# Reordering casts, gate products and exponentials in a fused hybrid decoder layer, and a seven-product form for its first pooling pair

## The chip, the cores and the metric

The kernel runs on one core of one Trainium2 chip. The metric is device time in microseconds (us), from launch to end; lower is better. A core has five engines that work side by side, each in the order of its own instruction queue: TensorE (PE in the profile, its weight loads PEld) multiplies matrices into PSUM, VectorE (DVE) and ScalarE (ACT) do elementwise work, GpSimd (POOL) does little but issue DMAs here, and SyncE (SP) issues DMAs. An instruction waits at the head of its queue until what it needs is there, and all behind it wait too.

## The reference

One decoder layer on 512 tokens and 16 leading meta tokens, width 1024, in float32:

```python
u = rmsnorm(h, mix_norm_w)
proj = u @ w_in                       # pool 1024, z 2048, x/B/C 4096, dt 32, gates 2048
y_pool = pool_mixer(u_pool, ...) @ w_pool_up
y_ssd = mamba2_branch(z, xbc, dt_raw, ...) @ w_ssd_out
h = h + (gate_pool * y_pool + gate_ssd * y_ssd) @ w_o
v = rmsnorm(h, mlp_norm_w)
h = h + relu(v @ w_ff1) ** 2 @ w_ff2
out = rmsnorm(h, final_norm_w)[:, 16:]
```

The Mamba branch has 8 groups of 256 channels. Each group goes through a causal convolution with silu (x, B, C), a chunked scan (four chunks of 128 tokens, with decays that are exponentials of running sums), a product with silu(z), and a norm over the group's 256 channels. The pooling branch has four groups with windows 2, 4, 8 and 16: the mean over the window minus the input, then a 256x256 product.

## The kernel before

Every float32 operand of TensorE is split into a high and a low part of a faster type. For weights, a block of 128x1024 is loaded by SP into a `raw` buffer, ACT casts it to the high half (`whi`, line 103), and DVE subtracts to get the low half (`wlo`, line 105). A product is then three matmuls: high times high, high times low input, low times high. There are four buffers for `whi`, four for `wlo` and three for `raw` (a fourth during the scan). A load waits until the low half of an older block has been taken, and a cast waits until TensorE has used up the high half of an older block.

The program is written with Python generators and a planner at compile time puts each engine's instructions into a fixed order, by the order of the text and by its own estimates of when operands are ready. `tc.issue_after(ins)` is a hint to that planner: the instructions in its block are placed behind `ins` in the queue of `ins`'s engine. It makes no wait of its own.

The scan part runs over the groups `g = 0..7`. `weave` (line 712) lets `ssd(g)`, the scan of one group, take turns with `group_proj(g + 1)`, the projections of the next group: first B and C (`plain`, lines 521 to 527), then x, then for three groups a pooling gate (`gate_pool`), then the two halves of z (`z_half`, line 529, into the PSUM tile `pz`). For groups 4 to 7 the x projection is a `pair` (line 480): two tiles of 256 channels are computed at once with seven half-size products instead of eight, in the order `b11 b21 t2 t1 s3 b22 t4`, on sums of the input that were prepared earlier (tiles `t0h`, `t1h` and their low parts) and on sums of the weights that GpSimd's DMAs accumulate in DRAM. The results of `pair` are combined by ACT and DVE from the PSUM tile `pqx` into `rax` and `rbx`.

`ssd(g)` is a generator of several steps: transposes of B and x (`ptb`, `ptm`, `ptx`), exponentials `eb` of the running sums and relus that prepare the decay mask (lines 612 to 626), the mask's exponentials (`decay`, line 627), the product of C and B (`pcb`, line 640), the chunk states (`st`, lines 656 and 657), the outputs (`po`, `py`, `yt`), the squares of the output (`sqg`) with their high and low half (`qhg`, line 319, and `qlg`, line 320), their sum over channels by TensorE (`png`, lines 693 and 694), and the normalized output's halves (`yh`, `yl`). Groups 0 to 3 also prepare the input's sums, in `sums_of_u` (line 876). With group 7 there is no next projection; `out_part` (line 822) takes its place and begins the branch's output projection (`psp`).

After the scan comes the pooling branch: `pool_tile` (line 931) for the two tiles of the first pool (window 16), products of the last two output blocks (`psl`), a gate, and `pool_pair` (line 963), the seven-product form, for the other three pools, where the weights' sums are made by DVE.

Of the kernel before, what the change touches and what calls it, by code (L numbers as in the profile page):

```python
# [64 lines left out]
def kernel(ctx: ExitStack, tc, xT, x, w, fx, f1, f2, vec, fnw, out):  # L65
# [32 lines left out]
        block_load(t, c)  # L98
        block_split(t, c)

    def block_split(t, c, behind=None):
        b, raw, hi, lo = t
        act.copy(hi[:, c], raw[:, c])  # L103
        with tc.issue_after(behind.ins) if behind is not None else nullcontext():
            dve.tensor_tensor(lo[:, c], raw[:, c], hi[:, c].bitcast(F32), op=ALU.subtract)  # L105

    def block(behind=None):
        t = block_tiles()
        block_load(t, slice(0, 1024))
        block_split(t, slice(0, 1024), behind)  # L110
        return t[2:]

    def raw_block():
# [82 lines left out]
        for o, c in outs:  # L196
            pe.matmul(o, wl, rhs[0][k][:, c], start=False, stop=k == NK - 1)

    def proj(outs, wblk, rhs):

        for part in range(2):
            for k in range(NK):
                wt = wblk[part][:, k * P : (k + 1) * P]
                for o, c in outs:
                    pe.matmul(o, wt, rhs[0][k][:, c], start=part == 0 and k == 0, stop=part == 1 and k == NK - 1)  # L205
                    if part == 0:
                        mm[0] = pe.matmul(o, wt, rhs[1][k][:, c], start=False, stop=False)  # L207

# [9 lines left out]
    def narrow(ps):  # L218
        return [(ps, slice(NM, L))]
# [95 lines left out]
    def col_sums(name, qt, n2, tags, bufs=1):  # L315

        qh = n2.tile(list(qt.shape), F32R, tag=tags[0], name=f"qh{name}", bufs=bufs)
        ql = n2.tile(list(qt.shape), F32R, tag=tags[1], name=f"ql{name}", bufs=bufs)
        act.copy(qh, qt)
        dve.tensor_tensor(ql, qt, qh.bitcast(F32), op=ALU.subtract)  # L320
        return qh, ql

# [138 lines left out]
    def pair_operands(i):  # L461
# [3 lines left out]
        for a in range(0, 7, 2):  # L465
# [11 lines left out]
            for j in range(len(ms)):  # L477
                yield hi[:, 512 * j : 512 * (j + 1)], lo[:, 512 * j : 512 * (j + 1)]

    def pair(kind, g, r):  # L480

        ps = psum2(f"pq{kind}{g}")
        banks = (ps[:, :HALF], ps[:, 512 : 512 + HALF])
        operands = pair_operands(PAIRS.index((kind, g)))
        one, two = HF
        for m, f, n, start, stop in MULTIPLY:
            o = banks[n]
            wt = next(operands)
            f = factor_u(f)
            for low in range(2):  # L490
                for k in range(4):
                    wk = wt[low][:, k * P : (k + 1) * P]
                    pe.matmul(o, wk, f[k][0], start=start and not low and k == 0,  # L493
                              stop=stop and low == 1 and k == 3, skip_group_check=True)
                    if not low:
                        pe.matmul(o, wk, f[k][1], start=False, stop=False, skip_group_check=True)
            if m == "b11":
                act.copy(r[0][:, one], o)
            elif m == "b21":
                dve.tensor_tensor(r[0][:, one], r[0][:, one], o, op=ALU.add)  # L500
            elif m == "t2":
                act.activation(r[1][:, one], o, AF.Copy, scale=-1.0)
            elif m == "t1":
                act.copy(r[1][:, two], o)
                yield
            elif m == "s3":
                dve.tensor_tensor(r[1][:, two], r[1][:, two], o, op=ALU.subtract)
            elif m == "b22":
                dve.tensor_tensor(r[1][:, one], r[1][:, one], o, op=ALU.add)
            else:  # L510
                act.copy(r[0][:, two], o)
# [4 lines left out]
    def group_proj(g, cur, gate=None):  # L516

        first = g == 0
        xc, bt, ct, zt = cur

        def plain(dst, t, skip):
            if first and (dst is bt or dst is ct):
                view = viewB if dst is bt else viewC
            else:
                runs, view = wide(psum2(f"px{g}_{t}"), skip)
                proj(runs, block(), X if first else U)
            conv(dst, first_raw(t, view, skip) if first else view, t)

        def z_half(ps, i):

            with tc.issue_after(done[0].ins) if g == 1 else nullcontext():
                wt = block()
            proj(narrow(ps), wt, X if first else U)

        bcs = ((bt, 16 + g, 0), (ct, 24 + g, NM - 4))
        xs = ((xc[:, 0, :], 2 * g, 0), (xc[:, 1, :], 2 * g + 1, 0))
        both = g in BC_PAIRS
        for kind, ts, paired in (("b", bcs, both), ("x", xs, g in X_PAIRS)):
            if paired:
# [37 lines left out]
    def ssd(g, cur):  # L577
# [31 lines left out]
        xdd = gs.tile([P, 3, R, 64], F32, tag="xdd", name=f"xdd{g}")  # L609
        x_decayed[g] = dve.tensor_tensor(xdd, xdt[:, :3, :, :], bc(dec[:, :3, hs], 64), op=ALU.mult)  # L610

        eb = gs.tile([P, 2, SEQ], F32, tag="eb", name=f"eb{g}")
        ap = abc.rearrange("p (i j) l -> p i j l", j=2)
        for j in range(2):
            js = slice(64 * j, 64 * j + 64)
            with tc.issue_after((z_ready if g in X_PAIRS else x_ready)[g].ins):
                act.activation(eb[js, :, :], ap[js, :, j, :], AF.Exp)
        dm = abc.rearrange("p r (c l) -> p r c l", c=4)
        for r in range(R):
# [15 lines left out]
        yield  # L635

        pc = psum1(f"pcb{g}")
        with tc.issue_after(filled[g].ins) if g in X_PAIRS and g in filled else nullcontext():
            for c in range(4):
                pe.matmul(pc[:, c * P : (c + 1) * P], bt[:, tok(c)], ct[:, ctok(c)], start=True, stop=True)  # L640
        cbm = gs.tile([P, 4, P], F32, tag="cbm", name=f"cbm{g}")
# [12 lines left out]
                decay()  # L654
        for c in range(3):
            dve.tensor_tensor(st[c + 1], st[c], bc(cdec[:, c, hs], 64), op=ALU.mult)
            dve.tensor_tensor(flat(st[c + 1]), flat(st[c + 1]), pv[c + 1], op=ALU.add)
        for rs_ in ((slice(0, 2), slice(2, R)) if g == G - 1 else (slice(0, R),)):
            n = rs_.stop - rs_.start
            masked[g] = dve.tensor_tensor(dm[:, rs_], dm[:, rs_], cbm.unsqueeze(1).to_broadcast([P, n, 4, P]),  # L660
# [25 lines left out]
        sq = gs.tile([P, 2, SEQ], F32, tag="eb", name=f"sqg{g}")  # L686
        squared[g] = act.activation(sq, yt, AF.Square)
        dve.tensor_tensor(sq[:, 0, :], sq[:, 0, :], sq[:, 1, :], op=ALU.add)
        qh, ql = col_sums(f"g{g}", sq[:, 0, :], gs, ("btok", "cbm"))
        mark[0] = qh.bitcast(F32)[:, :1]  # L690
        yield
        pn = psum1(f"png{g}")
# [14 lines left out]
            ys.append((yh, yl))  # L707
        yield

    done, abc_load, masked, y_first, squared, b_meta, x_decayed = {}, {}, {}, {}, {}, {}, {}  # L710

    def weave(a, b, n, sums, side):
# [109 lines left out]
    def out_part():  # L822

        def get(n):
            t = block_tiles()
            block_load(t, slice(0, 1024))

            with tc.issue_after(b_meta[G - 1].ins) if n == 1 else nullcontext():
                act.copy(t[2], t[1])
            with tc.issue_after(x_decayed[G - 1].ins) if n == 1 else nullcontext():  # L830
                dve.tensor_tensor(t[3], t[1], t[2].bitcast(F32), op=ALU.subtract)
            return t
# [43 lines left out]
    def sums_of_u(g):  # L876
# [11 lines left out]
            load(0)  # L888
        yield
        a, b = u_raw[g]  # L890
        with tc.issue_after(masked[g].ins):
            dve.tensor_tensor(b[:, two], a[:, two], b[:, two], op=ALU.subtract)
            dve.tensor_tensor(a[:, two], a[:, one], a[:, two], op=ALU.subtract)
            dve.tensor_tensor(a[:, one], b[:, two], a[:, one], op=ALU.subtract)
# [32 lines left out]
    pool_stack = ExitStack()  # L927
    gp = pool_stack.enter_context(tc.tile_pool(name="gp", bufs=2, side="right", reuse_waits="tile"))
    yps, last, copied, mixed = {}, {}, {}, []

    def pool_tile(t):
        win = WIN[t // 2]
        ps = psum2(f"pp{t}")

        skip = min(NM - win, NM - 4)
        runs, view = wide(ps, skip)
        proj(runs, block(), U)
        u = gp.tile([P, L + 8], F32, tag="pu", name=f"pu{t}", bufs=4)[:, :L]
        act.copy(u[:, skip:], view)
        return averaged(t, u)  # L940

    def averaged(t, u):
        win = WIN[t // 2]
# [92 lines left out]
    for _ in range(SETS_POOL):  # L1036
        with tc.issue_after(t_load.ins):
            t_load = weight_sums()
    pend = [pooled_halves(*pool_tile(2 * POOL_ORDER[0] + i)) for i in range(2)]

    un = units()
    psl_add = []
# [781 lines left out]
```

## Time and profile before

| what | value |
|---|---|
| time, median of 3 runs (lowest to highest) | 1010.49 us (1010.44 to 1011.99) |
| time of the profiled execution | 1010.66 us |
| span of its instructions | 1009.0 us |
| busy: PE, DVE, ACT, POOL | 993.8, 798.2, 604.8, 129.4 us |
| granted TensorE clock, mean of the span | 0.997 |

A line of the timeline gives the start in us from the span's start, the duration, the engine with the program line, the operation, output and inputs, and in brackets how long the engine had been idle before and what ended that. A line of the windows gives a stretch, its length, and for each engine asked for the busy time with the number of instructions, then the granted clock of TensorE (1.00 is full speed), the share of the DMA engines in use, and GB/s. Matmuls of one kind overlap in their pipeline, so that their distance and not their duration is what one costs.

### The profile page before, as it was taken

The page shows a single profiled execution, that of the slowest core. Times are in us where ns is not written, and L with a number is a line of the kernel's source. Part 1 is how long each engine was busy: PE and PEld are TensorE (multiplying, and loading weights), DVE is VectorE, ACT ScalarE, POOL GpSimd, SP SyncE. Part 2 cuts the span into 40 slices and gives each one's busy share as a digit, 9 for nine tenths or more (in the row PEclk, how much of TensorE's full clock was granted, in tenths as well). Part 3 has the DMA queues.
Part 4 walks back from the last instruction along what each step waited for, and adds up shares of the span by engine and source line. Part 5 has one row for each costly group of instructions (what it writes and reads, how often), then busy time and mean ns, then how long its engine had stood idle before and what let it go on. Part 6 is the DMA issues. An engine that isn't in the chain of part 4 may idle for free.

```text
span 1009.0 us, 15702 instructions
## 1 busy us (share of the span) xinstructions
PE 993.8 (98%) x6047; PEld 875.5 (87%) x6047; DVE 798.2 (79%) x1153; ACT 604.8 (60%) x853; POOL 129.4 (13%) x215
## 2 busy tenths in 40 slices
PE   9999999999999999999999999999999999999997
PEld 7889998998888898978999888888889999999986
DVE  7978897968754788988689657876988878888885
ACT  8657759494834566675345434368656656665654
POOL 0001331212122212213300000221000000000000
PEclk9999999999999999999999999999999999999999
DMA  7273958576889749478823631979355464554432
GB/s 250 90 262 100 314 175 218 170 207 201 225 226 271 211 129 276 138 210 203 258 94 122 225 124 64 290 197 345 86 190 154 137 200 135 167 173 153 135 106 83
DMA packets 61803, 184.52 MB, mean 183 GB/s; under 512 B 7072, under 2 KB 8416, under 8 KB 60704
## 3 DMA queue, kind: packets, MB, share of 16 engines
q1 hardware_dynamic: 39456, 109.00, 32.3%
q0 software_dynamic: 18240, 67.51, 26.0%
q10 hardware_dynamic: 4032, 7.00, 1.9%
q8 instruction: 47, 0.77, 0.3%
q14 instruction: 28, 0.23, 0.1%
HBM read 173.13 MB, written 58.59 MB: 230 GB/s over the span
## 4 chain that ended last, share of the span: by engine, by line
PE 90%; DVE 3%; ACT 3%; DMA 2%; issue 1%; SPq 0%; ACTq 0%; DVEq 0%
PE px L1443 8%; PE px L205 7%; PE alpha L1511 6%; PE pz L205 6%; PE px L1446 4%; PE px L207 3%; PE alpha L1514 3%; PE pz L207 3%; PE pgs L205 3%; PE pgp L205 2%; DMA raw<-in_w 2%; PE pqx L493 2%; PE pso L137 1%; PE wo_alpha L1205 1%; PE pf L138 1%; PE pf L137 1%
## 5 line engine op out<-in xcount | busy, mean ns | idle before, releaser
L103 ACT CAST whi<-raw 128x1024 fp32r<-128x1024 f32 (+2 forms) x90 | 90.0, 1011 | 87.5 <-DMA raw<-in_w 15.8
L105 DVE TENSOR_TENSOR wlo<-raw,whi 128x1024 fp32r<-128x1024 f32 (+2 forms) x90 | 104.7, 1172 | 37.6 <-ACT whi L103 21.1
L205 PE MATMUL px<-uh,whi 128*128 128x264 f32 (+1 forms) x320 | 80.9, 291 | 0.0
L207 PE MATMUL px<-ul,whi 128*128 128x264 f32 (+1 forms) x320 | 78.8, 285 | 0.0
L1218 DVE TENSOR_TENSOR ht<-ht,alpha 128x1024 f32<-128x1024 f32 x35 | 42.7, 1220 | 29.1 <-PE alpha L1511 29.1
L1141 ACT CAST shi<-rawf 128x1024 fp32r<-128x1024 f32 x42 | 44.2, 1053 | 28.7 <-PE alpha L1514 18.2
L205 PEld LDWEIGHTS px<-uh,whi 128*128 128x128 f32 x320 | 60.4, 189 | 1.1 <-issue 0.7
L207 PEld LDWEIGHTS px<-ul,whi 128*128 128x128 f32 x320 | 60.2, 188 | 0.2
L1511 PE MATMUL alpha<-shi,hh 128*128 128x512 f32 x140 | 55.2, 394 | 0.0
L1514 PE MATMUL alpha<-shi,hl 128*128 128x512 f32 x140 | 54.7, 391 | 0.0
L1142 DVE TENSOR_TENSOR slo<-rawf,shi 128x1024 fp32r<-128x1024 f32 x42 | 51.2, 1219 | 0.6 <-ACT shi L1141 0.6
L1446 PE MATMUL px<-vsl,shi 128*128 128x256 f32 x192 | 47.4, 280 | 0.0
L1443 PE MATMUL px<-vsh,shi 128*128 128x256 f32 x192 | 47.4, 281 | 0.0
L205 PE MATMUL pz<-uh,whi 128*128 128x512 f32 x112 | 44.2, 394 | 1.9 <-ACT yh L705 1.3
L207 PE MATMUL pz<-ul,whi 128*128 128x512 f32 x112 | 43.7, 390 | 0.0
L205 PE MATMUL px<-uh,wlo 128*128 128x264 f32 (+1 forms) x320 | 41.8, 283 | 0.0
L205 PEld LDWEIGHTS px<-uh,wlo 128*128 128x128 f32 x320 | 40.0, 188 | 0.2
L1511 PE MATMUL alpha<-slo,hh 128*128 128x512 f32 x140 | 37.4, 389 | 0.0
L698 DVE RECIPROCAL rs<-rs 128x128 f32<-128x128 f32 x32 | 27.2, 911 | 12.5 <-ACT rs L696 12.4
L1443 PEld LDWEIGHTS px<-vsh,shi 128*128 128x128 f32 x192 | 36.2, 188 | 0.9
L1446 PEld LDWEIGHTS px<-vsl,shi 128*128 128x128 f32 x192 | 36.1, 188 | 0.9
L1446 PE MATMUL px<-vl,shi 128*128 128x256 f32 x144 | 36.1, 283 | 0.0
(599 smaller groups left out, 3089.6 us busy)
## 6 DMA issues: line engine op xcount, KB each, us to landing
raw<-in_w SPq DMA_DIRECT2D x96, 512.0 KB, 4.6
f_t<-in_f POOLq DMA_DIRECT2D x38, 512.0 KB, 6.8
f_s<-in_f POOLq DMA_DIRECT2D x26, 512.0 KB, 7.0
b<-in_f SPq DMA_DIRECT2D x21, 512.0 KB, 4.6
rawf<-in_f SPq DMA_DIRECT2D x36, 256.0 KB, 3.0
rawf<-f_t SPq DMA_DIRECT2D x36, 256.0 KB, 2.9
abc<-acs_d POOLq DMA_DIRECT2D x8, 1024.0 KB, 7.6
f_t<-f_t POOLq DMA_DIRECT2D x12, 512.0 KB, 7.0
```

The costliest lines, as they stand in the source:

```text
L103: act.copy(hi[:, c], raw[:, c])
L105: dve.tensor_tensor(lo[:, c], raw[:, c], hi[:, c].bitcast(F32), op=ALU.subtract)
L205: pe.matmul(o, wt, rhs[0][k][:, c], start=part == 0 and k == 0, stop=part == 1 and k == NK - 1)
L207: mm[0] = pe.matmul(o, wt, rhs[1][k][:, c], start=False, stop=False)
L698: dve.reciprocal(rs[:, ctok(c)], rs[:, ctok(c)])
L1141: splits.append((act.copy(hi, src), dve.tensor_tensor(lo, src, hi.bitcast(F32), op=ALU.subtract)))
L1142: dve.tensor_tensor(lo, src, hi.bitcast(F32), op=ALU.subtract)))
L1218: added[0] = dve.tensor_tensor(o, o, src, op=op)
L1443: pe.matmul(ps, m, f[k][0], start=start and not low and k == 0, stop=stop and low == 1 and k == 3, skip_group_check=True)
L1446: pe.matmul(ps, m, f[k][1], start=False, stop=False, skip_group_check=True)
L1511: pe.matmul(ps[t], hh[:, p, seg, st], m, start=bool(first and not low and p == 0), stop=bool(last and low and p == 1), skip_group_check=True)
L1514: pe.matmul(ps[t], hl[:, p, seg, st], m, start=False, stop=False, skip_group_check=True)
```

## The change

Six edits, most of them hints to the planner; a small helper `after` takes several such hints at once:

- **z's casts**: for the three groups with a pooling gate among the projections (groups 2, 3 and 4), both casts of z's weights are placed behind `qhg` of the scan that runs beside them.
- **z's products**: for groups 4 to 7, the first matmul of z is placed behind the last matmul of the pair's third product (`t2`).
- **the last group's exponentials**: `ssd(7)` gets one more step, and its `eb` exponentials are placed behind the cast of `out_part`'s second weight block.
- **C times B**: `pcb` is placed behind the first projection of the next group for all groups that have one, and not only for groups 4 to 6.
- **sums of the input**: they are placed behind the last chunk state of the group, besides behind its mask.
- **the first pool** uses `pool_pair`; `pool_tile` goes away.

```diff
-    def block_split(t, c, behind=None):
+    def block_split(t, c, behind=None, cast_behind=None):
         b, raw, hi, lo = t
-        act.copy(hi[:, c], raw[:, c])
+        with after(cast_behind):
+            act.copy(hi[:, c], raw[:, c])
...
+    def proj(outs, wblk, rhs, behind=None):
...
-                    pe.matmul(o, wt, rhs[0][k][:, c], start=part == 0 and k == 0, stop=part == 1 and k == NK - 1)
+                    with after(behind if part == 0 and k == 0 else None):
+                        pe.matmul(o, wt, rhs[0][k][:, c], start=part == 0 and k == 0,
+                                  stop=part == 1 and k == NK - 1)
...
             elif m == "t2":
+                second_product[g] = at
...
             with tc.issue_after(done[0].ins) if g == 1 else nullcontext():
-                wt = block()
-            proj(narrow(ps), wt, X if first else U)
+                wt = block(None, halved.get(g - 1) if gate is not None else None)
+            proj(narrow(ps), wt, X if first else U, None if i else second_product.get(g))
...
+        if g == G - 1:
+            yield
         eb = gs.tile([P, 2, SEQ], F32, tag="eb", name=f"eb{g}")
...
-            with tc.issue_after((z_ready if g in X_PAIRS else x_ready)[g].ins):
+            with after((z_ready if g in X_PAIRS else x_ready)[g], late_cast[0] if g == G - 1 else None):
                 act.activation(eb[js, :, :], ap[js, :, j, :], AF.Exp)
...
-        with tc.issue_after(filled[g].ins) if g in X_PAIRS and g in filled else nullcontext():
+        with tc.issue_after(filled[g].ins) if g in filled else nullcontext():
...
-            dve.tensor_tensor(flat(st[c + 1]), flat(st[c + 1]), pv[c + 1], op=ALU.add)
+            last_state[g] = dve.tensor_tensor(flat(st[c + 1]), flat(st[c + 1]), pv[c + 1], op=ALU.add)
...
-        qh, ql = col_sums(f"g{g}", sq[:, 0, :], gs, ("btok", "cbm"))
+        qh, ql, halved[g] = col_sums(f"g{g}", sq[:, 0, :], gs, ("btok", "cbm"))
...
-            with tc.issue_after(b_meta[G - 1].ins) if n == 1 else nullcontext():
-                act.copy(t[2], t[1])
+            with after(b_meta[G - 1] if n == 1 else None):
+                cast = act.copy(t[2], t[1])
+            if n == 1:
+                late_cast[0] = cast
...
-        with tc.issue_after(masked[g].ins):
+        with after(masked[g], last_state[g]):
             dve.tensor_tensor(b[:, two], a[:, two], b[:, two], op=ALU.subtract)
...
-    pend = [pooled_halves(*pool_tile(2 * POOL_ORDER[0] + i)) for i in range(2)]
+    pend = [pooled_halves(*a) for a in pool_pair(POOL_ORDER[0])]
```

The pool pair, which the first pool now goes through, in its core:

```python
        a1, a2 = raw_block(), raw_block()
        fa = split_form(a1, both, f"A{p}")
...
            dve.tensor_tensor(sm[:, h1], a1[:, h1], a2[:, h1], op=ALU.add)
...
            dve.tensor_tensor(sm[:, h2], sm[:, h1], a2[:, h2], op=ALU.add)
        fs = split_form(sm, both, f"S{p}")
        dve.tensor_tensor(a1[:, h1], a2[:, h1], a2[:, h2], op=ALU.add)
        dve.tensor_tensor(a1[:, h2], a1[:, h2], sm[:, h2], op=ALU.add)
        fd = split_form(a1, both, f"D{p}")
        fb = split_form(a2, h2, f"B{p}")
...
        product(c, fa, 0, "A11", True, False)
        act.copy(r1[:, one], c)
        product(y, fa, 1, "A12", True, True)
        dve.tensor_tensor(r1[:, one], r1[:, one], y, op=ALU.add)
        product(c, fs, 1, "S2", False, False)
        act.activation(r2[:, one], c, AF.Copy, scale=-1.0)
        product(z, fs, 0, "S1", True, False)
        copied[p] = act.copy(r2[:, two], z)
        product(c, fd, 0, "S3", False, False)
        dve.tensor_tensor(r2[:, two], r2[:, two], c, op=ALU.subtract)
        product(z, fb, 1, "S4", False, True)
        dve.tensor_tensor(r2[:, one], r2[:, one], z, op=ALU.add)
        second = averaged(2 * p + 1, r2)
        product(c, fd, 1, "A22", False, True)
        act.copy(r1[:, two], c)
        return [averaged(2 * p, r1), second]
```

Each `product` is 4 input blocks times 3 matmuls of 264 columns; `pool_tile` had 8 input blocks times 3 matmuls times 2 runs of 264 columns for each of two tiles.

More of the change, by code (lines that the diff above doesn't have):

```diff
@@ L99, in block_part, with after, block @@
         block_split(t, c)
-    def block_split(t, c, behind=None):
+    def after(*ins):
+        st = ExitStack()
+        for i in ins:
+            if i is not None:
+                st.enter_context(tc.issue_after(i.ins))
+        return st
+    def block_split(t, c, behind=None, cast_behind=None):
         b, raw, hi, lo = t
-        act.copy(hi[:, c], raw[:, c])
+        with after(cast_behind):
+            act.copy(hi[:, c], raw[:, c])
         with tc.issue_after(behind.ins) if behind is not None else nullcontext():
             dve.tensor_tensor(lo[:, c], raw[:, c], hi[:, c].bitcast(F32), op=ALU.subtract)
-    def block(behind=None):
+    def block(behind=None, cast_behind=None):
         t = block_tiles()
         block_load(t, slice(0, 1024))
-        block_split(t, slice(0, 1024), behind)
+        block_split(t, slice(0, 1024), behind, cast_behind)
         return t[2:]
@@ L197, in proj_step @@
             pe.matmul(o, wl, rhs[0][k][:, c], start=False, stop=k == NK - 1)
-    def proj(outs, wblk, rhs):
+    def proj(outs, wblk, rhs, behind=None):
         for part in range(2):
@@ L318, in col_sums @@
         ql = n2.tile(list(qt.shape), F32R, tag=tags[1], name=f"ql{name}", bufs=bufs)
-        act.copy(qh, qt)
+        at = act.copy(qh, qt)
         dve.tensor_tensor(ql, qt, qh.bitcast(F32), op=ALU.subtract)
-        return qh, ql
+        return qh, ql, at
     NT = L // 6
@@ L478, in pair_operands @@
                 yield hi[:, 512 * j : 512 * (j + 1)], lo[:, 512 * j : 512 * (j + 1)]
+    second_product, halved = {}, {}
     def pair(kind, g, r):
@@ L492, in pair @@
                     wk = wt[low][:, k * P : (k + 1) * P]
-                    pe.matmul(o, wk, f[k][0], start=start and not low and k == 0,
-                              stop=stop and low == 1 and k == 3, skip_group_check=True)
+                    at = pe.matmul(o, wk, f[k][0], start=start and not low and k == 0,
+                                   stop=stop and low == 1 and k == 3, skip_group_check=True)
                     if not low:
@@ L708, in ssd @@
         yield
+    late_cast, last_state = [None], {}
     done, abc_load, masked, y_first, squared, b_meta, x_decayed = {}, {}, {}, {}, {}, {}, {}
@@ L929 @@
     yps, last, copied, mixed = {}, {}, {}, []
[L931 to L940, printed above, removed]
     def averaged(t, u):
```

## The prediction

> **What bounds the kernel now.** I read the first page, then who TensorE waits for, then the timelines around each of those waits. From the page:
>
> ```profile
> span 1009.0 us, 15702 instructions
> PE 993.8 (98%) x6047; PEld 875.5 (87%) x6047; DVE 798.2 (79%) x1153; ACT 604.8 (60%) x853; POOL 129.4 (13%) x215
> ```
>
> TensorE is busy 98% of the span, so time comes only from fewer matmuls or from the 15.2 us in which it is idle. The view of waits, for TensorE alone, lists nearly all of it that is not start or end:
>
> ```profile
> PE pqx L493 <- DVE rbx L509: 1.9, 1, 1.9
> PE png L693 <- ACT qhg L319: 1.6, 1, 1.6
> ```
>
> ```profile
> PE pz L205 <- ACT yh L705: 1.3, 1, 1.3
> PE psp L861 <- ACT whi L829: 1.2, 1, 1.2
> PE po L669 <- DVE st L657: 0.7, 1, 0.7
> PE pz L205 <- ACT rax L511: 0.5, 1, 0.5
> ```
>
> Each is a single wait of one place (the columns are the total, the count and the longest). Together they are 7.2 us, and the edits aim at these places. So each edit is priced by whether its wait goes, and by what is late next.
>
> **z's casts, group 2** (beside the scan of group 1). ScalarE, then VectorE:
>
> ```profile
> 146.26 1.06 ACT L687 ACTIVATE sqg<-yt 128x1024 f32<-128x1024 f32 x1 [2.91 <-DVE yt L682]
> 148.68 0.79 ACT L426 ACTIVATE xc<-px,vs 128x528 f32<-128x528 f32 x1 [1.35 <-PE px L205]
> 151.79 1.04 ACT L103 CAST whi<-raw 128x1024 fp32r<-128x1024 f32 x1 [2.32 <-DMA raw<-in_w]
> 152.74 0.61 ACT L319 CAST qhg<-sqg 128x512 fp32r<-128x512 f32 x1
> ```
>
> ```profile
> 146.14 2.36 DVE L105 TENSOR_TENSOR wlo<-raw,whi 128x1024 fp32r<-128x1024 f32 x2
> 148.41 0.69 DVE L688 TENSOR_TENSOR sqg<-sqg 128x512 f32<-128x512 f32 x1
> ```
>
> `qhg` could run at 149.10 (148.41 + 0.69) but stands behind a cast that waits 2.32 us for its load; `png` pays 1.6. Counted in the order of the blocks that cast is not z's but that of the next block, the first of group 3. I take it that casts keep the order of the blocks, since they share four buffers: if z's two casts go behind `qhg`, this one does too. Then `qhg` runs in ScalarE's idle time before 151.79, z's two casts (1.04 each) fit behind it until z's products at 154.9, and one of the two low halves of 146.14 no longer stands ahead of the squares' sum. The wait of 1.6 goes. Bounds: 0 (the cast at 151.79 stays ahead) to -1.6; I take **-1.6**. What the moved casts carry with them: the low halves come some 5 us later, so do the releases of two `raw` buffers and SP's loads behind them. Those loads are for blocks of group 3 that TensorE uses 20 us later, which covers them.
>
> Where it could hurt is ScalarE behind that point:
>
> ```profile
> 136.00:151.80 15.80, 4.95 (x7) 1.00 0.83 277
> ```
>
> ```profile
> 151.80:177.00 25.20, 24.98 (x33) 1.00 0.79 211
> 201.20:224.80 23.60, 22.77 (x31) 1.00 0.79 231
> ```
>
> ScalarE is idle 10.9 of the 15.8 us before and full for 25 us after (and again from 201.2, in group 3). So two casts of 1.04 cost nothing if `qhg` comes early, and 2.1 us each time if it does not. In group 3 no wait of TensorE is there to be won; I take 0.
>
> **z's casts, group 4.** ScalarE, VectorE and the granted clock (third number from the end):
>
> ```profile
> 248.40 1.05 ACT L103 CAST whi<-raw 128x1024 fp32r<-128x1024 f32 x1 [3.65 <-PE pqx L493]
> 249.35 0.61 ACT L319 CAST qhg<-sqg 128x512 fp32r<-128x512 f32 x1
> ```
>
> ```profile
> 254.41 1.04 ACT L103 CAST whi<-raw 128x1024 fp32r<-128x1024 f32 x1 [1.46 <-DMA raw<-in_w]
> 255.36 0.37 ACT L511 COPY rax<-pqx 128x264 f32<-128x264 f32 x1
> ```
>
> ```profile
> 250.60 0.42 DVE L509 TENSOR_TENSOR rbx<-rbx,pqx 128x264 f32<-128x264 f32 x1
> ```
>
> ```profile
> 252.00:254.00 2.00, 2.00 (x9) 0.50 1.03 377
> 254.00:256.00 2.00, 1.48 (x6) 0.65 0.88 295
> ```
>
> Here z's second cast does stand ahead of `qhg`; `qlg` and then `rbx` follow on VectorE, and TensorE waits 1.9. With `qhg` first, the pair's last product starts up to 1.9 us earlier. But z's products need the PSUM that the copy `rax` frees, and `rax` stands behind a cast whose load lands only at 254.41. The wait moves there. The half-speed stretch costs 1.7 us more (2 x 0.50 + 2 x 0.35); it follows the wait and would move with it. I take **0**. Bounds: -4.1 (1.9 + 0.5 + 1.7: `rax` also gets ahead) and +2.1 (z's two casts, now late, hold z's products up).
>
> The Trainium skill, TensorE: Matmul & The Clock Gate, section "What's actually happening", lets the clock fall to half only after an idle window of about 3.4 us. This case's trace has 0.50 after a wait of 1.9 us, so the row speaks against it as a threshold for single waits; by that rule the moved wait would cost no clock and the sum would be 1.7 us lower, which is the third rival.
>
> **z's products, group 5.**
>
> ```profile
> 324.60 1.23 DVE L105 TENSOR_TENSOR wlop<-rawp,whip 128x1024 fp32r<-128x1024 f32 x1 [4.61 <-PE px L205]
> ```
>
> ```profile
> 333.71 0.64 PE L493 MATMUL pqx<-uh,wlop 128*128 128x264 f32 x4
> 335.62 0.47 PE L205 MATMUL pz<-uh,whi 128*128 128x512 f32 x1 [1.26 <-ACT yh L705]
> ```
>
> ```profile
> 334.73 0.74 DVE L429 SCALAR_TENSOR_TENSOR ct<-px,vs,ct 128x512 f32<-128x512 f32 x1
> ```
>
> z's first matmul stands after the pair's second product and waits; the convolution of C still reads the PSUM until 335.47. The third product's weights were split by 325.83 and it needs none of this. At 12 matmuls it takes about 1.5 us (12/84 of the 10.19 shown below), more than the wait of 1.26. Behind it z is ready. In groups 6 and 7 z already starts after the third product, in group 4 after the whole pair. **-1.3**, bounds 0 and -1.3.
>
> **The last group's exponentials.** ScalarE:
>
> ```profile
> 442.55 1.28 ACT L617 ACT_TABLE_LOAD   x1
> 443.85 2.14 ACT L617 ACTIVATE eb<-abc 64x1024 f32<-64x1024 f32 x2
> ```
>
> ```profile
> 449.41 1.03 ACT L829 CAST whi<-raw 128x1024 fp32r<-128x1024 f32 x1
> ```
>
> ```profile
> 450.61 1.06 ACT L628 ACTIVATE abc<-abc 128x1024 f32<-128x1024 f32 x1
> ```
>
> ```profile
> 453.69 1.07 ACT L849 COPY sp<-psp 128x512 f32<-128x512 f32 x2
> ```
>
> The cast on which `psp` waits 1.2 moves ahead of the `eb` exponentials, to about 442.6. ScalarE has the same work, so the mask's exponentials stay near 450.6. Late next: the copies `sp` at 453.69, that free PSUM, and the mask's products, both behind those exponentials until 452.6. TensorE can win what lies between; I take **-1.0**, bounds 0 (ScalarE, full, hands it back) and -1.2. The extra step also lets GpSimd's weight-sum DMAs of this stretch start at other marks; they are needed hundreds of us later: 0.
>
> **C times B, and the sums of the input.** In the chain, group 3:
>
> ```profile
> 219.82 1.93 PE px L205 x16
> 221.76 0.91 PE pcb L640 x8
> ```
>
> `pcb` already follows the whole first projection, so the hint changes nothing where it is. The sums are four VectorE steps of 0.42 (the row of `rbx`, same shape) that go behind the states; the one wait on a state is the 0.7 above. Both **0**, bounds -0.7 and +0.7.
>
> **The first pool.** TensorE now, and for a pair of today (group of window 8):
>
> ```profile
> 484.08:495.74 11.66, 11.66 (x97) 1.00 0.89 264
> 514.79:524.98 10.19, 10.19 (x85) 1.00 0.27 98
> ```
>
> 96 matmuls of 264 columns become 84: 11.66 - 10.19 = 1.47 less. VectorE gets four sums of 0.69, low halves of 3 x 1.23 + 0.69 in place of 2 x 1.23, and three additions of 0.42: 2.8 + 1.9 + 1.3 = 6.0 us more. Its room:
>
> ```profile
> 466.00:484.00 18.00, 12.23 (x16) 1.00 0.91 207
> 484.00:495.60 11.60, 4.73 (x6) 1.00 0.90 263
> 495.60:514.00 18.40, 17.64 (x24) 1.00 0.48 167
> ```
>
> 5.8 + 6.9 us are idle before 495.6 and 0.8 after. Loads, casts and sums can go in the first part, but both windowed means (five steps of 0.69 each) now end after the pair, where VectorE is full and the gate's and next pair's low halves queue behind them. I leave 0.5 for that: **-1.0**, bounds -1.5 and +4.5 (all 6.0 come late).
>
> **Sum.** -1.6 + 0 - 1.3 - 1.0 + 0 - 1.0 = -4.9. The profiled execution took 1010.66 (its span and 1.7 around it): 1005.8. It lies 0.17 above the median of 1010.49, so the forecast for the median is **1005.6**, with a range of its own of 1004.2 to 1007.6.
>
> **Rivals.**
> First, the ScalarE edits give nothing: the cast at 151.79 keeps its place, and the cast of group 7 only moves its wait to `sp`. For: ScalarE is full in both stretches. Against: before 151.79 it is idle. Left: -1.3 - 1.0, 1008.2. Chance 0.21, half of it within 0.2% of before.
> Second, slower: z's casts crowd ScalarE. Place: behind `qhg` in groups 2, 3 and 4. Price: 2.1 us in each, as the mask, the states and z's products come that much later: +6.3, with the 1.6 of group 2 not won and -3.3 from the rest: 1013.5. It decides by whether `qhg` runs before 151.8 and 201.2, ahead of the full stretches. Chance 0.16.
> Third, group 4 gives more: 1.7 (the clock stays full, the rule named above) to 4.1: 1003.9 to 1001.5. For: the load that lands at 254.41 would share the DMA engines with one load less, as the next waits for z's low half. Against: the clock row. Chance 0.13.
> Fourth, the planner's new order opens waits elsewhere that take back the 4.9, each hint doing what it says and nothing more: 1010.5, chance 0.10.
>
> **How the numbers follow.** Forecast 0.40, rivals 0.21, 0.16, 0.13, 0.10. Within 0.2% (2 us, about what a measurement of this kernel can tell): 0.10 + 0.10 = 0.20; faster 0.40 + 0.11 + 0.13 = 0.64; slower 0.16. The range 1002.3 to 1012.0 leaves out the larger part of the slower rival and the far end of the third.
>
> **What would show it.** Right: the rows of waits for `png` (1.6), `pz` on `yh` (1.3) and `psp` on `whi` (1.2) are gone; `qhg` of group 1 starts before 150; some wait of 2 us stays near z's products of group 4, with a clock near 0.5; the first pool's products span about 10.2 us. Wrong: `qhg` still behind a cast with a DMA named, new rows of waits on `st`, `abc` or `po` in groups 2 and 3, or TensorE waiting on `pl`, `wlo` or `pu` between 495 and 515.

## The result, and the profile after

The changed kernel takes 1014.55 us (median of 5 runs, 1013.43 to 1015.87) beside 1010.49 for the kernel before (1010.1 to 1012.52): a ratio of 1.0036, 95% interval 1.0020 to 1.0052. It is slower, where I had forecast 1005.6. The profiled execution took 1013.97, its span is 1012.3 against 1009.0.

The first page of the changed kernel:

```profile
span 1012.3 us, 15679 instructions
PE 992.1 (98%) x6035; PEld 874.9 (86%) x6035; DVE 804.3 (79%) x1162; ACT 604.9 (60%) x856; POOL 122.7 (12%) x215
```

TensorE has 12 matmuls less and is busy 1.7 us less (992.1 against 993.8), yet the span is 3.3 us longer: its idle time grew by 5. The view of waits, TensorE alone, says where (line numbers have moved by some 10 to 30; L214 is a projection's first matmul, L111 the cast of a weight block):

```profile
PE px L214 <- ACT whi L111: 5.7, 1, 5.7
...
PE pqx L505 <- DVE rax L512: 1.5, 1, 1.5
PE psp L145 <- ACT sp L867: 1.4, 1, 1.4
PE pqx L505 <- ACT rax L510: 1.4, 1, 1.4
PE po L684 <- DVE st L672: 0.9, 1, 0.9
```

The four waits that the change aimed at (`pqx` on `rbx` 1.9, `png` on `qhg` 1.6, `pz` on `yh` 1.3, `psp` on `whi` 1.2) are gone. In their place stand three of about the same size and one of 5.7 that is new. This one is the first matmul of group 3, and it waits for the cast of its weights. ScalarE around it:

```profile
149.71 0.62 ACT L329 CAST qhg<-sqg 128x512 fp32r<-128x512 f32 x1 [0.76 <-DVE sqg L703]
150.24 2.00 ACT L111 CAST whi<-raw 128x1024 fp32r<-128x1024 f32 x2
...
158.09 2.15 ACT L632 ACTIVATE eb<-abc 64x1024 f32<-64x1024 f32 x2
...
169.22 1.04 ACT L643 ACTIVATE abc<-abc 128x1024 f32<-128x1024 f32 x1
170.17 1.98 ACT L111 CAST whi<-raw 128x1024 fp32r<-128x1024 f32 x2
```

`qhg` now runs at 149.71 and z's two casts right behind it, as forecast. But the next cast, of group 3's first block, which stood at 151.79 before, comes at 170.17, behind both sets of exponentials of group 2's scan and all that ScalarE does between them, with no idle time ahead of it. TensorE was free for it at 165.52. The granted clock (third number from the end) falls meanwhile:

```profile
166.00:168.00 2.00, 0.00 (x0) 0.00 (x0) 1.37 (x2) 1.98 (x4) 0.67 (x2) 0.94 0.79 96
168.00:170.00 2.00, 0.00 (x0) 0.00 (x0) 0.00 (x0) 1.99 (x3) 0.00 (x0) 0.50 1.00 215
170.00:172.00 2.00, 0.75 (x3) 0.75 (x4) 0.77 (x1) 2.00 (x3) 0.00 (x0) 0.50 0.52 213
172.00:174.00 2.00, 2.00 (x11) 2.00 (x10) 2.00 (x3) 2.00 (x3) 0.00 (x0) 0.50 0.36 47
174.00:176.00 2.00, 2.00 (x16) 2.00 (x15) 1.86 (x2) 0.04 (x1) 0.00 (x0) 0.85 0.90 324
```

TensorE works from 171.25 on, at half speed until about 174.6 (clock 0.85 over 174 to 176 is 0.6 us at 0.50 and the rest full): 1.7 us more.

Step by step, as time between the same landmarks of both profiles (z's last product of each group, then TensorE's last `png`, its first `pf`, the end):

| stretch | forecast | after minus before |
|---|---|---|
| to the end of group 1 | 0 | +0.70 |
| group 2 | -1.6 | -2.77 |
| group 3 | 0 | +7.62 |
| group 4 | 0 | -2.90 |
| group 5 | -1.3 | +0.57 |
| groups 6, 7, last scan | -1.0 | -0.27 |
| pools, to the first `pf` | -1.0 | -0.75 |
| the rest | 0 | +1.11 |
| sum | -4.9 | +3.31 |

Some 0.6 to 0.8 us of group 2's gain is no gain: six of group 2's transposes stood ahead of z's products (153.75 to 154.32 before) and now stand behind, in the next stretch.

### The profile page after: what moved, and what is told of

It reads as the page before. It is cut to its first block, busy times and chain, and to the rows that moved or that the text cites. A ratio compares the mean times of both kernels' runs of the same rounds, so it can differ in the third digit from the quotient of the medians.

```text
span 1012.3 us, 15679 instructions
## 1 busy us (share of the span) xinstructions
PE 992.1 (98%) x6035; PEld 874.9 (86%) x6035; DVE 804.3 (79%) x1162; ACT 604.9 (60%) x856; POOL 122.7 (12%) x215
## 4 chain that ended last, share of the span: by engine, by line
PE 90%; ACT 5%; DVE 2%; DMA 2%; issue 1%; ACTq 0%; DVEq 0%
PE px L1450 8%; PE px L214 7%; PE alpha L1518 6%; PE pz L214 6%; PE px L1453 4%; PE px L217 4%; PE alpha L1521 3%; PE pgp L214 3%; PE pz L217 3%; PE pgs L214 3%; PE pqx L505 3%; DMA raw<-in_w 2%; PE pso L145 1%; PE pgp L217 1%; PE pso L146 1%; PE pso L148 1%
## 5 line engine op out<-in xcount | busy, mean ns | idle before, releaser
L113 DVE TENSOR_TENSOR wlo<-raw,whi 128x1024 fp32r<-128x1024 f32 (+2 forms) x88 | 101.7, 1170 | 43.7 <-ACT whi L111 25.7
L111 ACT CAST whi<-raw 128x1024 fp32r<-128x1024 f32 (+2 forms) x88 | 87.5, 1010 | 74.8 <-DMA raw<-in_w 17.8
L214 PE MATMUL px<-uh,whi 128*128 128x264 f32 (+1 forms) x320 | 82.4, 295 | 5.7 <-ACT whi L111 5.7
L214 PEld LDWEIGHTS px<-uh,whi 128*128 128x128 f32 x320 | 61.5, 192 | 7.1 <-ACT whi L111 6.0
L214 PE MATMUL pz<-uh,whi 128*128 128x512 f32 x112 | 43.9, 392 | 0.0
L214 PE MATMUL px<-uh,wlo 128*128 128x264 f32 (+1 forms) x320 | 41.8, 283 | 0.0
L214 PEld LDWEIGHTS px<-uh,wlo 128*128 128x128 f32 x320 | 39.9, 188 | 0.0
```

## The experiments

All kernels compute the whole result. Each was timed beside runs of the kernel before, and the ratio is to those (their medians were 1012.05 to 1012.58, single runs 1009.5 to 1016.9; the change's 1014.55 is 0.2% over these medians too). Spans and waits are those of one profiled execution each. The letters: A z's casts behind `qhg`; B z's products behind the third product; C the last group's exponentials behind a cast; D C times B behind the next group's first projection; E the sums of the input behind the last state; F the first pool pair. D alone needs no run: the order of instructions is then the same on every engine as before.

The order in which each engine is given its instructions is fixed when the kernel is built, and it was the clue to the first theory: with A alone, three casts stand behind `qhg` of group 1, the third being that of group 3's first block; with A and E together only two do. So my **first theory** was that E, together with A, displaced that cast. The rivals: ScalarE has no room for the casts (**theory 2**), or z's low halves, which now come late, hold up the load of that block (**theory 3**).

### Without E

```
-        with after(masked[g], last_state[g]):
+        with after(masked[g]):
```

> The change without the hint that puts the sums of the input behind the last state (edit E). Theory 1 (that hint, together with the casts of z behind the squares' high half, put the first cast of group 3 behind ScalarE's exponentials): without it this cast stands straight behind the two casts of z, ahead of the exponentials, the wait of 5.73 us of px is gone, and the time is that of the forecast, 1005.6, between 1004.2 and 1008. Theory 2 (z's casts crowd ScalarE wherever they stand): a wait of px or pz of 4 us or more on a cast stays near 155 to 175 us, and the time is over 1012. Theory 3 (z's low halves, now late, hold up the load of that block): the cast stands early but waits for its load, px waits 2 to 4 us and the time is 1009 to 1011.

Measured: ratio 1.0021 (1.0012 to 1.0031), span 1012.8. In group 2 all is as that theory had it: the wait of `png` is gone, 0.52 is left ahead of z's products. But the same wait stands one group later, TensorE's largest, and ScalarE's order there shows why:

```profile
PE px L214 <- ACT whi L111: 6.2, 1, 6.2
```

```profile
199.81 0.62 ACT L329 CAST qhg<-sqg 128x512 fp32r<-128x512 f32 x1 [1.28 <-DVE sqg L703]
200.33 1.04 ACT L111 CAST whi<-raw 128x1024 fp32r<-128x1024 f32 x1
201.28 0.64 ACT L441 ACTIVATE xc<-xc 128x528 f32<-128x528 f32 x1
201.83 1.03 ACT L111 CAST whi<-raw 128x1024 fp32r<-128x1024 f32 x1
```

z's two casts stand behind `qhg`, then no weight cast until 220.25, again behind both sets of exponentials; TensorE waits for it from 215.09 to 221.33. So the first theory falls: E doesn't make the fault, it moves it from group 4's first block to group 3's.

### A alone

```
+                wt = block(None, halved.get(g - 1) if gate is not None else None)
```

> The kernel before with the casts of z behind the squares' high half alone. Theory 1: no wait of px in group 3's first block, the wait of png (1.56) gone, group 4's waits changed by -4.1 to +2.1: 1005 to 1010, most likely 1008.9. Theory 2 and theory 3: as in the full change, a wait of 4 us or more before group 3: 1013 to 1016.

Measured: 0.9983 (0.9968 to 0.9999), span 1008.5. The wait of `px` is there, at 218.82 in group 4's first block, but it is 2.14 and not 6.2: TensorE does C times B and the state products ahead of it (with waits of 0.52 and 0.43 of their own). A's gains are there as well: group 2 takes 1.7 less.

### E alone

```
+        with after(masked[g], last_state[g]):
```

> The kernel before with the sums of the input behind the last state alone. Theory 1: it does its harm only with the casts of z; the first cast of group 3 stands behind the squares' high half and ahead of the exponentials, so no wait of 5 us; 1009 to 1012. A rival that blames this hint alone: the wait of 5.73 us is here too, 1014 to 1016. Under either, the 0.7 us that the change loses in group 0 (waits of po and py at 86 to 91 us) should show here, and not in the two kernels without the hint.

Measured: 0.9983 (0.9970 to 0.9996), span 1009.6. No wait of 5 us, as both my first theory and its successor have it. But E isn't neutral in place: `py` and `po` of group 2 now wait 1.48 and 0.92, `pqx` of group 4 2.31, while the old waits of `png` and `rbx` are gone by the new order. The 0.9 of `po` in group 0 is here, but also in the kernel with A alone, so it isn't E's: to the end of group 1 the kernels of this study stand 0.1 to 1.1 behind the profile of before, with E and without it (one, with a stretch of half speed at 24 us, 2.5).

### The change without A

```
-                wt = block(None, halved.get(g - 1) if gate is not None else None)
+                wt = block(None, None)
```

> The change without the casts of z behind the squares' high half. Theory 1: no wait of 5 us before group 3; what is left is the sums' hint (+0.7 in group 0), z's products (0 to -1.3), the last group (0 to -1.2) and the pool (-1.0 to -1.5): 1007 to 1010.5. Theory 2: also 1007 to 1010.5. The rival that blames the sums' hint alone: over 1013.

Measured: 0.9990 (0.9975 to 1.0004), span 1012.1. The wait of 5 us is gone, and the ratio is lower than the change's; only the one profile is no shorter, since the wait of 1.76 of `py` that E brings halved the clock for 6.8 us in it. This leaves **theory 4**: A, which holds back z's casts, lets the first cast of the next group fall behind the exponentials of the scan that runs beside; the place of that one cast is the price, and D, which forbids TensorE to do C times B before that projection, makes it larger.

### The cast put ahead of the exponentials

All six edits, and group 3's first block taken from the loop, ahead of group 2's scan:

```
     for g in range(G):
+        if g in (2,):
+            ahead[g + 1] = block()
...
-                proj(runs, block(), X if first else U)
+                proj(runs, ahead.pop(g) if g in ahead else block(), X if first else U)
```

> The full change, with the block of group 3's first projection taken from the loop ahead of group 2's scan, so that ScalarE's order has its cast ahead of the exponentials; loads, buffers and all six edits are the same. Theory 4 (the casts of z push the first cast of the next group behind the exponentials of the scan; the place of that one cast is the price): the wait of 5.73 us and the half-speed stretch behind it (some 1.2 us) go, the span falls by 5 to 7 us from 1012.3, and the time is 0.1 to 0.4% under before. Theory 3 (its load is late): the cast waits for its load until after 164 and px still waits over 2 us; the span falls by less than 4. Theory 2 (ScalarE has no room): the exponentials end 1 us later and py or po of group 2 takes over the wait; the span falls by less than 3.

Measured: 0.9967 (0.9954 to 0.9980), span 1007.4, 4.9 less than the change and just under the 5 to 7 expected. ScalarE:

```profile
156.93 0.69 ACT L711 ACTIVATE rs<-png,eps 128x512 f32<-128x512 f32 x1
157.51 1.04 ACT L111 CAST whi<-raw 128x1024 fp32r<-128x1024 f32 x1
158.57 1.28 ACT L632 ACT_TABLE_LOAD   x1
159.87 2.15 ACT L632 ACTIVATE eb<-abc 64x1024 f32<-64x1024 f32 x2
```

The cast runs at 157.51 with no wait for its load (theory 3 would show a DMA in brackets), some 7 us before TensorE comes to it (166.11). The exponentials come later, and no wait of `py` or `po` in group 2 answers (theory 2). The edit moves one cast of 1.04 us up by about 13 us; the planner then changes the places of some steps behind it too (z's activation, relus, later casts). Group 3's stretch goes from +7.62 to +0.13, and the kernel from slower than before to faster.

### Without D

```
-        with tc.issue_after(filled[g].ins) if g in filled else nullcontext():
+        with tc.issue_after(filled[g].ins) if g in X_PAIRS and g in filled else nullcontext():
```

> The full change without the hint that puts C times B behind the next group's first projection in all groups (edit D). Theory 4 with a second part (D forbids TensorE to do C times B and the states while px waits for that cast): the cast stays behind the exponentials, but C times B and the state products fill part of the time, the wait of px falls from 5.73 to 2 to 3 us, and the span falls by 2.5 to 4.5 from 1012.3. The rival, by which D does nothing, as the forecast had it: the wait stays at 5.7 and the span within 1 us of 1012.3.

Measured: 0.9984 (0.9971 to 0.9998), span 1008.1: 4.2 less. The cast still stands behind the exponentials, but the waits are

```profile
PE px L214 <- ACT whi L111: 1.6, 1, 1.6
...
PE pst L664 <- DVE xdd L623: 0.6, 1, 0.6
```

and the clock stays full. TensorE does C times B at 165.94 and the state products behind it up to 170.2, in the time in which the change waits. D does nothing alone, and costs 4.2 us here, where the projection that it waits for is late.

### Without E, with group 4's cast put ahead

> The change without the sums' hint, with the block of group 4's first projection taken ahead of group 3's scan. Theory 4: the wait of 6.24 us that the kernel without the sums' hint has at 215 goes with its half-speed stretch, the wait of png stays gone, and what is left against before is z's products (+0.2), the last group (+0.4) and the pool (-1.0 to -1.5): a span of 1004.5 to 1007.5, 0.15 to 0.45% under before. A rival, that casts and exponentials together are simply more than ScalarE can do there: another wait of 2 us or more between 215 and 260, and a span over 1009.

The same edit with `(3,)`, and E left out. Measured: 1006.16 us, 0.9934 (0.9913 to 0.9955), span 1004.9. TensorE's waits:

```profile
...
PE pqx L505 <- DVE rax L512: 1.5, 1, 1.5
PE psp L145 <- ACT sp L867: 1.4, 1, 1.4
PE po L684 <- DVE st L672: 0.8, 1, 0.8
```

The wait of 6.2 is gone, and with it theory 2. This version beats both kernels: it gains about the 4.9 that I had forecast (its span is 4.1 under before in one profile, the ratio of the times 0.66% or 6.7 us under), though from other terms. Behind the kernel's start, the two largest rows are those that B and C left.

### B, C and F alone

> The kernel before with z's products behind the third product (B), the last group's exponentials behind a cast (C) and the first pool pair of seven products (F), which act in three stages far apart. As the forecast had it, B -1.3, C -1.0, F -1.0: a span of 1005.7. As the profile of the change suggests, B's wait of 1.26 becomes one of 1.5 of the pair's next product on VectorE's addition, C's wait of 1.2 becomes one of 1.4 on the copies out of PSUM, and F alone gains 1.0 to 1.5: a span of 1007.8 to 1008.8.

Measured: 0.9998 (0.9981 to 1.0015). The waits:

```profile
PE pqx L505 <- DVE rbx L522: 2.1, 1, 2.1
PE png L708 <- ACT qhg L329: 1.7, 1, 1.7
...
PE pqx L505 <- DVE rax L512: 1.5, 1, 1.5
PE psp L145 <- ACT sp L867: 1.4, 1, 1.4
```

The upper two are those of before. B's 1.26 has become 1.5, C's 1.20 has become 1.44, as the second expectation had it. The span is not: 1014.0, since the clock fell to half in three places of this execution, behind the waits of 1.7, 2.1 and 1.4. By stretches, F gains 1.40.

### A in group 4 alone

```
-                wt = block(None, halved.get(g - 1) if gate is not None else None)
+                wt = block(None, halved.get(g - 1) if gate is not None and g == 4 else None)
```

> The kernel before with the casts of z behind the squares' high half in group 4 alone. The forecast took 0 here, since the wait of 1.86 would move to the copy out of the pair's PSUM. The profiles of the kernels without the sums' hint speak for its third rival: both waits (1.86 and 0.52) go, and with them the half-speed stretch of 1.7 where the run has one; everything ahead of 225 us stays as before. Span 1005 to 1007, 0.15 to 0.4% under before. By the forecast: within 0.1% of before, with a wait of about 2 us by 250.

The edit is shown against A alone. Measured: 1007.59 us, 0.9953 (0.9936 to 0.9969), span 1007.4, a little over the 1005 to 1007 expected: the wait of `png` in group 2, which is left as it was, is 1.80 here and halves the clock at 155.30, as it did not in the profile of before. Group 4 takes 4.5 us less; the wait of 1.9 and that of 0.5 are both gone. ScalarE behind `qhg` (247.91), then VectorE:

```profile
248.44 1.05 ACT L111 CAST whi<-raw 128x1024 fp32r<-128x1024 f32 x1
249.56 0.83 ACT L436 ACTIVATE xc<-rbx,vs 128x528 f32<-128x528 f32 x1
250.30 1.03 ACT L111 CAST whi<-raw 128x1024 fp32r<-128x1024 f32 x1
251.33 0.38 ACT L524 COPY rax<-pqx 128x264 f32<-128x264 f32 x1
252.55 1.05 ACT L111 CAST whi<-raw 128x1024 fp32r<-128x1024 f32 x1 [0.83 <-DMA raw<-in_w]
```

```profile
249.10 0.43 DVE L522 TENSOR_TENSOR rbx<-rbx,pqx 128x264 f32<-128x264 f32 x1 [1.22 <-PE pqx L505]
249.44 0.69 DVE L330 TENSOR_TENSOR qlg<-sqg,qhg 128x512 fp32r<-128x512 f32 x1
```

`rbx` no longer stands behind `qlg`, and `rax` stands ahead of the cast that waits for its load, where it stood behind it before. Nothing in group 4 waits, and the clock stays full there.

### The change without A in group 2

> The full change without the hint on z's casts in group 2 alone (groups 3 and 4 keep it). Theory 4: the cast of group 3's first block keeps its place ahead of the squares, so the wait of 5.73 goes; the waits of py and po in group 2 that the sums' hint gives without those casts (1.76 and 0.91 in the kernel without any of the casts' hints) may come in its place. Span 1005.5 to 1009.5. If the wait of over 4 us is still there, theory 4 has the wrong casts.

Measured: 0.9975 (0.9964 to 0.9987), span 1008.9. With `g != 2` in the same condition, the wait of 5.7 is gone; the waits of `py` (1.59) and `po` (0.91) that E brings stand in its place.

### A in groups 2 and 4, and F

> The kernel before with the casts' hint in groups 2 and 4 (not 3) and the first pool pair of seven products. Theory 4: no first cast stands behind exponentials, png's wait is down to about 0.5, group 4 gains 2 to 4, the pool 1.1 to 1.4: span 1002.5 to 1005, 0.4 to 0.7% under before. If casts and exponentials are simply too much for ScalarE: a wait of 2 us or more between 215 and 260 and a span over 1006.

Measured: 0.9989 (0.9973 to 1.0006), span 1009.7: a miss. The order that comes out for group 3 has the opposite fault:

```profile
204.12 1.05 ACT L111 CAST whi<-raw 128x1024 fp32r<-128x1024 f32 x1 [4.63 <-DMA raw<-in_w]
```

A cast that stands right behind `qhg`, ahead of its load, holds ScalarE idle for 4.63 us. At 229 to 233 `po` and `py` wait 1.0 and 1.8 and the clock halves. That the one leads to the other was not tried.

### A and F, with group 4's cast put ahead

> The kernel before with the casts' hint in all three groups, the first pool pair of seven products, and the block of group 4's first projection taken ahead of group 3's scan; against the kernel without the sums' hint with that block taken early, edits B, C and D are left out. As B and C only exchanged waits (1.26 for 1.50, 1.20 for 1.44), leaving them out gives 0.3 to 0.6 and, where a wait of 1.44 halves the clock, 1.5 more: span 1002.5 to 1004.6. If D or B or C carried a gain there: over 1005.

Measured: 1008.01 us, 0.9958 (0.9942 to 0.9974), span 1005.0: over the 1002.5 to 1004.6 expected, and at the 1005 over which I would have said that B, C or D carries a gain. Without B and C, group 5's stretch is 0.3 shorter than in the kernel with them, and the last scan 1.3, as the clock stays full; the pool is 1.2 longer. Whether B, C and D are worth anything beyond that is not shown. This one and the kernel with them have intervals that touch, so which of the two is better stays open. F gained nothing here. ScalarE in the pool:

```profile
486.35 1.04 ACT L111 CAST whi<-raw 128x1024 fp32r<-128x1024 f32 x1 [2.44 <-DMA raw<-in_w]
487.30 0.37 ACT L1009 COPY pu<-pz 128x264 f32<-128x264 f32 x1
```

The copy that frees the pair's PSUM stands behind a cast that waits 2.44 for its load, and the pair's next product pays 1.32.

## Why the prediction was wrong

**The step that failed** is what A's casts carry with them. For group 2 the prediction looked at the low halves and the loads, found both covered, and bounded the edit by "0 (the cast at 151.79 stays ahead) to -1.6", with no price on the other side; group 3's stretch then stands in the sum with 0. The cast itself is passed over in "I take it that casts keep the order of the blocks ... if z's two casts go behind `qhg`, this one does too. Then `qhg` runs in ScalarE's idle time". Casts did keep the order of blocks, and `qhg` did run early (149.71; 150.54 with the cast put ahead). What I did not ask is what the next cast may fall behind, once it has to follow z's. Behind z's casts lie 18.0 us of ScalarE's work without a gap (152.14 to 170.17), the same full stretch from 151.8 that I had quoted as a risk of 2.1. In the change the cast of group 3's first block landed at the end of it: 5.73 of wait and 1.7 at half clock, +7.62 in that stretch against 0 forecast. Putting that one cast ahead takes 4.9 us back, and leaving A out in group 2 alone removes the wait too, so it is group 2's hint, with E beside it, that makes it.

**D**: "the hint changes nothing where it is". True alone, and wrong with A: without D the change's span is 4.2 less. I priced the hint in the old order only, where `px` came first anyway.

**The slower rival** gave 1013.5, near the measured 1014.55, with the right engine and stretch. Its mechanism was another: three times 2.1, each by crowding. One late cast did it, in one group; with casts and exponentials in another order the same work fits. That the number came near is luck.

**Group 2, -1.6**: right. `png`'s wait went in every kernel with A there; 0.52 ahead of z's products is left without E, and the stretch takes 1.7 less with A alone. In the change itself the gain can't be put down to A, since that wait goes with E alone too.

**Group 4, 0**: wrong, and the third rival right in its size. I had `rax` behind "a cast whose load lands only at 254.41. The wait moves there". The order changed as a whole: `rax` went ahead of that cast, so it no longer matters to it when the load lands (the rival's reason), and the stretch takes 3.5 (A and F with the cast put ahead) to 4.5 less (A there alone). The forecast's far end was 4.1. In the change itself only 2.9 of it is left, as E adds a wait of 1.4 on `rax` at 241.13.

**B, -1.3**: wrong. "The third product's weights were split by 325.83 and it needs none of this." It does need something: the PSUM that VectorE's addition still reads. VectorE in the changed kernel:

```profile
337.68 0.74 DVE L439 SCALAR_TENSOR_TENSOR ct<-px,vs,ct 128x512 f32<-128x512 f32 x1
338.34 0.42 DVE L512 TENSOR_TENSOR rax<-rax,pqx 128x264 f32<-128x264 f32 x1
```

The addition stands behind C's convolution, the same that held z. Waiting for z (1.26) had hidden it; now it is waited for by itself (1.50). Group 5's stretch is -0.05 to +0.31 in kernels without B and +0.29 to +1.24 with it.

**C, -1.0**: the row late next was named (`sp`), the size wrong. ScalarE in the changed kernel:

```profile
455.69 1.05 ACT L644 ACTIVATE abc<-abc 128x1024 f32<-128x1024 f32 x1
456.64 1.04 ACT L867 COPY sp<-psp 128x512 f32<-128x512 f32 x2
```

The copies still stand behind the second exponential. The cast went ahead, the exponentials came after it, and TensorE waits 1.43 where it waited 1.20: -0.25 with a full clock, +1.33 in the three profiles where that wait halved it.

**F, -1.0**: right in size where nothing is in the way: -1.40, -1.20 and -1.14, with a wait of `pz` on the copy `pu` of 0, 0 and 0.07. The term that I left for VectorE (0.5) was ScalarE's: with a wait of 0.45 (the change) F gains 0.75, with 1.04 0.18, with 1.32 nothing.

**E, 0**, with bounds of 0.7 from the one wait on a state: wrong in both directions. It opens waits of 1.0 to 2.3 (`py`, `rax`) and closes others.

**Still open**: what decides, when the engines' orders are fixed, in which group a cast is put behind the exponentials. The orders were read, not the reason. Of the +1.11 behind the first `pf`, 0.9 and 1.1 show in two of the profiles with other edits too, and it was not traced.

## What to carry to other kernels

When a hint holds an instruction back, price not it but the next ones of its kind: follow each to the place that it can fall to in its engine's order, and charge the whole run of work ahead of that place, if a consumer is due before the end of it. A hint that changes nothing in today's order is still a bound: ask what the other edits make late, and whether it then forbids the work that would fill the wait. Where a wait goes, look for the next release of the same PSUM or buffer, and quote its row; B and C exchanged 1.2 for 1.4.

## What the runs showed of the hardware

The same wait may or may not cost the clock. The wait of `psp` on `sp`, once with the cast put ahead (1.44) and once without D (1.46), in the windows behind it (they began at 450.22 and 452.30):

```profile
452.00:454.00 2.00, 2.00 (x15) 1.60 (x16) 2.00 (x3) 1.98 (x3) 1.71 (x2) 0.69 0.43 20
454.00:456.00 2.00, 2.00 (x13) 1.67 (x10) 2.00 (x5) 0.00 (x0) 0.00 (x0) 0.50 1.12 150
456.00:458.00 2.00, 2.00 (x13) 1.66 (x11) 1.37 (x2) 0.19 (x1) 0.00 (x0) 0.95 0.87 235
```

```profile
454.00:456.00 2.00, 2.00 (x20) 1.34 (x19) 2.00 (x3) 2.00 (x3) 1.80 (x2) 1.00 0.46 29
456.00:458.00 2.00, 2.00 (x12) 1.74 (x12) 2.00 (x5) 0.09 (x1) 0.00 (x0) 1.00 1.07 133
```

The missing clock of the first three rows is 2 x (0.31 + 0.50 + 0.05) = 1.72 us, so 3.4 us at half speed; behind the wait of 5.73 above it is 2 x (0.06 + 3 x 0.50 + 0.15) = 3.4, so 6.8 us. The half-speed stretches of the other profiles, away from the start and end of the span, are 3.4 or 6.8 us too. Over all profiles of this case, no wait up to 1.3 us halved the clock by itself, every one over 2.0 did, and of those from 1.4 to 2.0 eight of 29 (from 60 us on). With 1.7 us for each stretch of 3.4, this is much of why runs of one kernel differ by several us, and why a single profile can hide a gain: of the 29 runs of before that stood beside the kernel with the cast put ahead, the nine with a mean clock of 0.999 or 1.000 took 1009.5 to 1012.4, the four at 0.993 to 0.995 took 1014.9 to 1016.9.

The moments at which the clock changes lie on a grid of 3.413 us in each profile (before: at 6.21, 251.97, 255.38 and 1006.32, which is 0, 72, 73 and 293 steps). Laid on that grid, from 60 us on, each of the ten full-speed steps in which TensorE idled for 1.7 us or more in all was followed by half speed, and none with under 1.4 was; of the 18 with 1.4 to 1.7, three were. So the wait of 1.99 in the change without A, which a step's end cuts into 1.58 and 0.41, cost nothing, and the 1.76 of `py` did, with 0.7 more in its step.

The Trainium skill, TensorE: Matmul & The Clock Gate, section "What's actually happening", has an activity window of 3.4 us that runs freely, not from the start of the kernel. The stretches of 3.4 and 6.8 us agree, and so does the grid. It does not explain the pair above, as both of those waits lie wholly inside one step. That a whole idle window is needed doesn't agree: 1.44 us of wait, with TensorE busy on both sides, was enough.
